# Attention scores computed transposed with the query maxima as an extra row, and convolution taps summed by GpSimd in the projections

## The chip, the cores and the metric

The kernel runs on one core of a Trainium2 chip. The core has five engines with queues of their own: TensorE (PE, matrix products, whose weight loads are PEld), VectorE (DVE), ScalarE (ACT), GpSimd (POOL) and SyncE (SP, which here only issues DMAs). They meet only through semaphores. The metric is the device time of one execution in microseconds. Measured before: a median of 2285.3 us over 3 runs (2282.73 to 2285.51).

## The reference

A two-layer encoder over 1024 tokens of width 1024, in float32. Each layer mixes tokens by latent attention of 8 heads beside a convolution over 31 positions on 512 channels, and then runs a gated feed-forward part with a convolution over 3 positions. Cut to what matters here:

```python
for l in range(DEPTH):
    h = _rmsnorm(x, g_mix[l])
    p = h @ w_in[l]
    q = (_rmsnorm(p[..., :o1], g_q[l]) @ w_uq[l]).reshape(b, s, MLA_HEADS, 64 + 32)
    kv = (_rmsnorm(p[..., o1:o2], g_kv[l]) @ w_ukv[l]).reshape(b, s, MLA_HEADS, 64 + 64)
    # q_rope, k_rope: the last 32 of q and p[..., o2:o3], rotated
    sc = einsum("bqhd,bkhd->bhqk", q_nope, k_nope) + einsum("bqhr,bkr->bhqk", q_rope, k_rope)
    y_attn = einsum("bhqk,bkhd->bqhd", softmax(sc * scale, axis=-1), v)
    a, gt = jnp.split(p[..., o3:], 2, axis=-1)
    u = _dwconv(a * sigmoid(gt), w_dw_conv[l], b_dw_conv[l])      # 31 taps
    u = silu(_layernorm(u, g_conv_ln[l], b_conv_ln[l]))
    x = x + concatenate([y_attn, u], axis=-1) @ w_o[l]
    z = _dwconv(_rmsnorm(x, g_ffn[l]) @ w_up[l], w_dw_ffn[l], b_dw_ffn[l])   # 3 taps
    zg, zv = jnp.split(z, 2, axis=-1)
    x = x + (silu(zg) * zv) @ w_down[l]
return _rmsnorm(x, g_final)
```

## The kernel before

Everything is kept transposed: channels on the 128 partitions, 1024 tokens along the free dimension. Each float32 operand of a product is split into an upper part, rounded to the PE's float32r format, and the remainder, and a product is three matmuls: upper by upper, upper by lower and lower by upper. The split is made by a cast on ACT and a subtraction on DVE. The order of PE, DVE, ACT and POOL is written out by hand; DMAs are issued from SP's queue (`move`) or from POOL's.

**Projections** (`project`, lines 516 to 819). The loop at line 801 walks through sections: gates and values of the convolution (four channel groups of 128), the latent parts, shared key, keys, rotated and plain queries. Each section's result stands in one of three two-bank PSUM tiles until DVE and ACT have taken it out. A planner keeps two clocks, PE's and DVE's: `work` (529) lets DVE do what a section needs as it falls due and fills the rest with taps of the 31-position convolution (`conv_step`, 1692: one multiply-add over 1024 tokens, 112 in all, NEAR_TAPS of 30 for each group). The other taps of a group are in `away`. Some go to `tap_far` (1697) in the longer sections: ACT multiplies, and a DMA from POOL's queue adds the product to the group's sum. Weights come in by DMAs on POOL's queue too: `cast` (161) loads the upper part, `complete` (177) has ACT negate it and adds the source by a second DMA (L174, L179). At the end queries and keys, upper and lower, go to DRAM, by head.

**Attention** (`attention`, 1469 to 1683). `load_head` brings back the four tiles of a head, queries and keys with 96 rows each. The main loop (1644) makes 64 steps, eight query tiles of eight heads. A step `n` issues: `scores` (1492) with queries as weights, six matmuls into a tile of 128 queries by 1024 keys, and DVE's maximum over the row; `expo` (1505), ACT's exponential with that maximum as bias and the row sum as a by-product; `turn` (1514), eight PE transposes a step of 128 by 128, since the product with the values needs keys on the partitions, with ACT's cast and DVE's subtraction of each half out of PSUM; and `values` (1537), four matmuls a step. `sums` (1567) turns a head's row sums, takes reciprocals and spreads them over 64 partitions by two DMAs through DRAM; POOL multiplies and splits the heads' results. `rows` (1476) makes the values' tiles at the start. The taps still in `away`, 49 a layer, are done during the steps by `tap_late` (1703): POOL or ACT multiplies, and POOL or a DMA adds. `early` and `finish` start the output product (`wo_steps`, 876) in the last steps.

PSUM has eight banks. In attention two two-bank tiles hold scores and four single banks the transposes, values and small things. SBUF tiles come from tagged pools: 31 of "b", 8 of "m" (heads' queries and keys), 3 of "wr" (exponentials), 8 of "ws".

**Feed-forward** (`feed`, 843) follows, and hands the next layer's first sections over.

## Time and profile before

| | |
|---|---|
| median of 3 runs | 2285.3 us |
| profiled execution, span from first to last instruction | 2282.9 us (the page gives no other time for it) |
| layer 0: projections, stretch 40 to 199 us | 159 us |
| layer 0: rows and attention, 199 to 424 us | 225 us |
| layer 1: rows and attention, 1326 to 1554 us | 228 us |
| granted TensorE clock | 0.999 |
| matmuls of scores, values, transposes (both layers) | 768, 512, 1024 |

The page gives busy time by engine, a strip of 40 slices, DMA queues, the chain that ended last, and the costliest groups of instructions. Matmuls overlap, so that the mean of one (389 ns) is longer than the distance from one to the next; the pitch is read from starts. In a tile's or line's rows the three figures are the shortest, median and longest duration in ns. In a timeline, two instructions merged into a row ("x2") have one duration for both. Idle time of an engine counts only where others wait for it.

### The profile page before, as it was taken

Reading aid. Unit: us, or ns where it says so; the run is one execution under the profiler, and the core shown is the slowest. Engines: PE = TensorE matmul, PEld = TensorE weight load, DVE = VectorE, ACT = ScalarE, POOL = GpSimd, SP = SyncE. Lnnn points to the kernel's source line nnn. Section 1 sums busy time; section 2 is a strip of 40 time slices with the busy share of each in tenths; the row PEclk is TensorE's granted clock in tenths of the full one; section 3 lists DMA queues with packets and bytes.
Section 4 is the critical chain, followed back from the end, with each engine's and each line's share of the span. In section 5 each row is a group of like instructions: output and inputs, shape, how many; then the busy total and the mean of one; then the engine's idle time right before and its main releaser. Section 6 shows DMA issues by size and latency. Waiting matters only on the chain.

```text
span 2282.9 us, 30530 instructions
## 1 busy us (share of the span) xinstructions
PE 2269.7 (99%) x10684; PEld 1887.8 (83%) x10684; DVE 1730.2 (76%) x2329; ACT 1286.7 (56%) x2043; POOL 781.8 (34%) x810
## 2 busy tenths in 40 slices
PE   9999999999999999999999999999999999999998
PEld 7888888888888888888888888888888888888887
DVE  6989888768877776776559788886697777768665
ACT  5445877646655555544533468774475555555444
POOL 1222787522333333001412237873323333320032
PEclk9999999999999999999999999999999999999999
DMA  6889998946899998935968999967659999989356
GB/s 185 165 175 271 194 200 166 235 138 145 211 277 296 275 296 208 334 106 143 209 136 166 218 255 197 184 149 207 175 129 228 271 302 279 294 210 315 102 124 167
DMA packets 198569, 475.73 MB, mean 208 GB/s; under 512 B 27296, under 2 KB 34576, under 8 KB 198416
## 3 DMA queue, kind: packets, MB, share of 16 engines
q0 software_dynamic: 103136, 222.46, 48.5%
...
## 4 chain that ended last, share of the span: by engine, by line
PE 92%; DVE 3%; DMA 1%; POOL 1%; ACT 1%; issue 1%; SPq 0%; DVEq 0%; ACTq 0%; POOLq 0%
PE p L1063 36%; PE pd L1251 18%; PE s L1500 7%; PE po L874 7%; PE o L1552 4%; PE t L1529 4%; PE pa L215 2%; PE pg L215 2%; PE pg L513 2%; DVE conv L1694 2%; PE pq L215 1%; PE pn L215 1%; PE pv L1481 1%; PE pkv L215 1%; PE pa L513 1%
## 5 line engine op out<-in xcount | busy, mean ns | idle before, releaser
L1063 PE MATMUL p<-b,w 128*128 128x512 f32 x3552 | 806.3, 389 | 0.1
L1063 PEld LDWEIGHTS p<-b,w 128*128 128x128 f32 x3552 | 666.4, 188 | 139.3 <-DVE w L1441 0.5
L1251 PE MATMUL pd<-ab,wd 128*128 128x512 f32 (+1 forms) x1920 | 422.3, 381 | 0.0
L1251 PEld LDWEIGHTS pd<-ab,wd 128*128 128x128 f32 x1920 | 350.7, 188 | 69.5 <-DVE ab L1441 0.4
L1500 PE MATMUL s<-k,q 96*128 96x512 f32 x768 | 208.0, 406 | 0.0
L179 POOL DMA_DIRECT2D w<-wu x96 | 84.7, 883 | 360.0 <-ACT w L178 319.1
L1532 DVE TENSOR_TENSOR pt<-t,pt 128x512 fp32r<-128x512 f32 x256 | 164.8, 685 | 53.6 <-ACT pt L1531 51.7
L1711 POOL TENSOR_TENSOR late<-gate,par 128x1018 f32<-128x1018 f32 (+12 forms) x79 | 171.7, 2174 | 18.7 <-issue 9.7
L1531 ACT CAST pt<-t 128x512 fp32r<-128x512 f32 x256 | 137.6, 589 | 65.2 <-PE t L1529 63.6
L1453 DVE SCALAR_TENSOR_TENSOR o<-zg,par,o 128x1023 f32<-128x1023 f32 x88 | 112.7, 1283 | 75.6 <-ACT o L1447 74.3
L179 POOL DMA_DIRECT2D w<-in_w_up x116 | 100.5, 866 | 199.4 <-ACT w L178 175.4
L1502 DVE TENSOR_REDUCE mx<-s 128x1 f32<-128x1024 f32 x128 | 155.8, 1217 | 0.0
L1500 PEld LDWEIGHTS s<-k,q 96*128 96x128 f32 x768 | 135.1, 189 | 22.9 <-ACT p L1510 0.2
L1510 ACT ACTIVATE p<-s,mx 128x1024 f32<-128x1024 f32 x128 | 144.8, 1131 | 1.9 <-DVE mx L1502 1.9
L1694 DVE SCALAR_TENSOR_TENSOR conv<-gate,par,conv 128x1009 f32<-128x1009 f32 (+7 forms) x112 | 142.3, 1274 | 3.6 <-ACT conv L575 1.0
L1552 PE MATMUL o<-pt,v 128*128 128x512 f32 x512 | 140.3, 397 | 0.0
L837 POOL DMA_DIRECT2D wd<-in_w_down x44 | 32.6, 744 | 307.9 <-PE pd L1251 306.9
L1439 ACT CAST ab<-ac 128x512 fp32r<-128x512 f32 x130 | 80.1, 617 | 98.3 <-DVE ac L1186 95.6
L178 ACT ACTIVATE w<-w 128x512 fp32r<-128x512 f32 x212 | 133.6, 630 | 3.0
L1529 PEld LDWEIGHTS t<-ident,p 128*128 128x128 f32 x1024 | 119.6, 140 | 18.5 <-ACT p L1510 1.2
L1529 PE MATMUL t<-ident,p 128*128 128x128 f32 x1024 | 133.3, 273 | 0.7 <-ACT p L1510 0.7
L1012 DVE TENSOR_TENSOR zg<-p,zg 128x512 f32<-128x512 f32 x88 | 60.5, 690 | 96.5 <-PE p L1063 89.6
...
## 6 DMA issues: line engine op xcount, KB each, us to landing
w<-in_w_up POOLq DMA_DIRECT2D x232, 256.0 KB, 7.2
...
w<-wu POOLq DMA_DIRECT2D x96, 256.0 KB, 5.9
...
wd<-in_w_down POOLq DMA_DIRECT2D x88, 256.0 KB, 5.3
...
ac<-act SPq DMA_DIRECT2D x72, 256.0 KB, 6.1
```

What stands on the lines that cost most here:

```text
L179: self.nc.gpsimd.dma_start(out=lo, in_=src, accum_op=ALU.add)
L215: nc.tensor.matmul(ps[:, HALVES[c]], w, x[:, HALVES[c]], start=(k == 0 and s == 0), stop=(k == n - 1 and s == 2))
L874: self.nc.tensor.matmul(ps, p[:, sl], q[:, cs], start=(k == 0 and t == 0), stop=(k == 3 and t == 2))
L1063: nc.tensor.matmul(ps, w[p][:, k * 128:(k + 1) * 128], b[:, q], start=(i in (1, 5, 2) and k == 0 and t == 0), stop=(k == 3 and t == 2), sk ...
L1251: nc.tensor.matmul(ps[t, m][:, cs], w[i, j][p][:, m * 128:(m + 1) * 128], b[:, q, cs], start=(i in (1, 5, 2) and j == 0 and s == 0), stop= ...
L1500: nc.tensor.matmul(ps[:, cs], q[i][0:96, qs], k[j][0:96, cs], start=(s == 0), stop=(s == 2))
L1502: nc.vector.tensor_reduce(out=mx, in_=ps, op=ALU.max, axis=AX.X, negate=True)
L1529: nc.tensor.transpose(tp[:, i, qi * 128:(qi + 1) * 128], st["p"][2 * qp + qi][:, kt * 128:(kt + 1) * 128], self.ident)
L1532: nc.vector.tensor_tensor(out=lo, in0=tp, in1=hi.bitcast(F32), op=ALU.subtract)
L1552: nc.tensor.matmul(po, v[2 * c + i][:, h // 2, e, :], pt[s][:, i, :], start=(c == 0 and i == 0 and s == 0), stop=(c == 3 and i == 1 and s ...
L1694: self.nc.vector.scalar_tensor_tensor(out=y[:, lo:hi], in0=u[:, lo + s:hi + s], scalar=self.tap(l, j, t), in1=y[:, lo:hi], op0=ALU.mult, o ...
L1711: self.nc.gpsimd.tensor_tensor(out=p[:, lo:hi], in0=u[:, lo + s:hi + s], in1=self.tap(l, j, t).broadcast_to([128, hi - lo]), op=ALU.mult)
```

## The change

In attention the score product is transposed: keys are the weights and queries move, so that a tile of 128 keys by 1024 queries comes out, with keys on the partitions as the value product needs them. PE's transposes go. The maximum of each query is found ahead of time from the upper parts alone (`peak`): two matmuls for every eighth query of a head, and DVE's maximum. A head's eight maxima go to DRAM and come back as row 96 of the query tile, beside a row of ones in the key tile, so that the last of the three score products subtracts them (97 rows). The exponential then needs no bias. It lies in SBUF, where ACT casts it (`cast`), DVE subtracts (`rest`: both operands in SBUF) and POOL adds the eight tiles of a head (`add`). `sums` turns these into row sums by eight matmuls with a column of ones. `peak` runs 12 steps ahead of the values, and 12 maxima come before the first scores, between the `rows`. Upper and lower tiles of a head are loaded apart. Head 1 gets its upper tiles directly, like head 0.

In the projections POOL takes taps from the end of `away` (`pool_tap`), up to ten for each group as the planner's clock allows, 3.4 us each: a product by a new one-operand form (`pool_product`) and an addition to the group's side sum, which one DMA adds to the group's sum in the end. What is left is done late, in turn by POOL and ACT, and in both cases added by a DMA. Four blocks of the output product instead of two begin in the last steps. The core of the diff (in `peak` to `sums`, in `spread` and `divide` and in the loop the removed lines are left out; they stand above):

```diff
-LATE_KINDS = (("pool", "both", "act", "pool", "act"), ("pool", "both", "pool", "pool", "pool"))
-LATE_COST = {"act": 1.1, "pool": 3.5, "both": 4.8}
+LATE_KINDS = ("pool", "act", "pool", "act")
+LATE_FROM = 0
+POOL_TAP = 3.4
+POOL_TAPS = (10, 10, 10, 10)
...
-DIRECT = 1
+DIRECT = 2
...
-        krd = [self.dp.tile([ROPE, T], F32R, name=f"krd{l}{i}") for i in range(2)]
+        krd = [self.dp.tile([ROPE + 1 - i, T], F32R, name=f"krd{l}{i}") for i in range(2)]
...
-            self.move(krd[0], krh[0:32, :])
+            self.move(krd[0][0:ROPE], krh[0:32, :])
+            self.move(krd[0][ROPE:ROPE + 1].rearrange("o (a b) -> (o a) b", a=8), self.ones_r[0:8, :])
...
+        pool_at, side = 0.0, {"j": 0, "n": 0}
+
+        def pool_tap():
+            j, y = side["j"], side.get("y")
+            t = away[j].pop()
+            lo, hi, s = self.span(t)
+            p = self.blk(f"side{l}_{j}_{t}")
+            if y is None:
+                side["y"] = p
+                if hi - lo < T:
+                    edge = p[:, hi:T] if hi < T else p[:, 0:lo]
+                    nc.gpsimd.memset(edge, 0.0)
+            self.pool_product(p[:, lo:hi], u[j][:, lo + s:hi + s], self.tap(l, j, t))
+            if y is not None:
+                nc.gpsimd.tensor_tensor(out=y[:, lo:hi], in0=y[:, lo:hi], in1=p[:, lo:hi], op=ALU.add)
+            side["n"] += 1
+            if side["n"] == POOL_TAPS[j] or not away[j]:
+                pool_merge()
+
+        def pool_merge():
+            j, y = side["j"], side.pop("y")
+            nc.gpsimd.dma_start(out=conv[j], in_=y, accum_op=ALU.add)
+            side.update(j=j + 1, n=0)
...
-            for j in sorted(far, key=far_at.get)[:FAR_TOGETHER if times[name] > 5.0 else 0]:
+            chosen = sorted(far, key=far_at.get)[:FAR_TOGETHER if times[name] > 5.0 else 0]
+            while pool_at + POOL_TAP <= clock["pe"] and away.get(side["j"]):
+                pool_at = max(pool_at, clock["pe"] - times[name]) + POOL_TAP
+                pool_tap()
+            for j in chosen:
                 self.tap_far(l, j, away[j].pop(0), u[j], conv[j])
...
+        if "y" in side:
+            pool_merge()
...
-        with self.psum(f"attn{l}", 2, 4):
+        with self.psum(f"attn{l}", 0, 2):
...
-            ms = (2 * i, 2 * i + 1) if n else ()
+            ms = (2 * i, 2 * i + 1) if n > 1 else ()
...
+    def upper_tiles(self, l, h):
+        return [self.tmp("m", f"{n}{l}_{h}0", F32R) for n in "qk"]
+
+    def lower_tiles(self, l, h):
+        return [self.tmp("m", f"q{l}_{h}1", F32R), self.tmp("ws" if h else "b", f"k{l}_{h}1", F32R)]
+
+    def load_part(self, l, h, p, qd, qrd, kd, krd):
+        q, k = tiles = self.lower_tiles(l, h) if p else self.upper_tiles(l, h)
+        self.move(q[0:NOPE, :], qd[p][h])
+        for i in range(2):
+            self.move(q[NOPE + i * HALF:NOPE + (i + 1) * HALF, :], qrd[p][i, h])
+        self.move(k[0:NOPE, :], kd[p][h])
+        rows = ROPE if p else ROPE + 1
+        self.move(k[NOPE:NOPE + rows, :], krd[p][0:rows])
         return tiles
...
+        def wide(name, tag):
+            return self.pp.tile([128, T], F32, name=name, tag=tag, bufs=2 if tag == "st" else 1)
...
+        def peak(h, i, tag="sm"):
+            st = state[h]
+            if i == 0:
+                st["mx"] = self.cp.tile([128, 8], F32R, name=f"mx{l}_{h}", tag="mx", bufs=2)
+            q, k = upper[h]
+            ps = wide(f"m{l}_{h}_{i}", tag)
+            for cs in HALVES:
+                nc.tensor.matmul(ps[:, cs], q[0:96, i::8], k[0:96, cs], start=True, stop=True)
+            nc.vector.tensor_reduce(out=st["mx"][:, i:i + 1], in_=ps, op=ALU.max, axis=AX.X, negate=True)
+            if i == 7:
+                self.move(md[h].rearrange("(p i) -> p i", i=8), st.pop("mx"))
+                self.move(q[96:97, :], md[h:h + 1])
+
         def scores(n):
+            h, kt = divmod(n, 8)
+            (qh, kh), (ql, kl) = upper[h], lower[h]
+            ks = slice(kt * 128, kt * 128 + 128)
+            ps = state[h]["s", kt] = wide(f"s{l}_{h}_{kt}", "st")
+            for s, (k, q, rows) in enumerate(((kh, ql, 96), (kl, qh, 96), (kh, qh, 97))):
+                for cs in HALVES:
+                    nc.tensor.matmul(ps[:, cs], k[0:rows, ks], q[0:rows, cs], start=s == 0, stop=s == 2)
+            if kt == 7:
+                upper.pop(h), lower.pop(h)
+
+        def expo(n):
+            h, kt = divmod(n, 8)
             st = state[h]
+            p = st["p", kt] = self.tmp("b" if kt % 4 == 3 else "wr", f"p{l}_{h}_{kt}")
+            nc.scalar.activation(out=p, in_=st.pop(("s", kt)), func=AF.Exp)
+
+        def cast(n):
+            h, kt = divmod(n, 8)
             st = state[h]
+            st["pt", kt] = [self.tmp("ws", f"pt{l}_{h}_{kt}{i}", F32R) for i in range(2)]
+            nc.scalar.copy(out=st["pt", kt][0], in_=st["p", kt])
+
+        def rest(n):
+            h, kt = divmod(n, 8)
             st = state[h]
+            hi, lo = st["pt", kt]
+            nc.vector.tensor_tensor(out=lo, in0=st["p", kt], in1=hi.bitcast(F32), op=ALU.subtract)
+
+        def add(n):
+            h, kt = divmod(n, 8)
             st = state[h]
+            if kt == 0:
+                return
+            if kt == 1:
+                st["acc"] = self.blk(f"acc{l}_{h}")
+            a = st.pop(("p", 0)) if kt == 1 else st["acc"]
+            nc.gpsimd.tensor_tensor(out=st["acc"], in0=a, in1=st.pop(("p", kt)), op=ALU.add)
+
+        def values(n):
+            h, kt = divmod(n, 8)
+            st, e = state[h], h % 2
+            if kt == 0:
+                st["po"] = [self.bank(f"o{l}_{h}_{c}") for c in range(2)]
+                if e == 0:
+                    st["y"], st["rb"] = self.blk(f"yt{l}_{h}"), self.blk(f"rb{l}_{h}")
+                else:
+                    st["y"], st["rb"] = state[h - 1]["y"], state[h - 1]["rb"]
+            pt = st.pop(("pt", kt))
+            for c, cs in enumerate(HALVES):
+                for s in range(2):
+                    nc.tensor.matmul(st["po"][c], v[kt][:, h // 2, e, :], pt[s][:, cs],
+                                     start=kt == 0 and s == 0, stop=kt == 7 and s == 1)
+
+        def sides(h):
             e = h % 2
+            return slice(e * 64, e * 64 + 64), slice(64 - e * 64, 128 - e * 64)
+
+        def gather(h, c):
+            main, aux = sides(h)
+            y, ps = state[h]["y"][main, HALVES[c]], state[h]["po"][c]
+            nc.scalar.copy(out=y, in_=ps[aux, :])
+            nc.vector.tensor_tensor(out=y, in0=ps[main, :], in1=y, op=ALU.add)
+
+        def sums(h):
+            st = state[h]
+            (main, _), acc = sides(h), st.pop("acc")
+            ps = wide(f"sr{l}_{h}", "st" if h == last else "sm")[:, 0:8]
+            for i in range(8):
+                cols = slice(i * 128, i * 128 + 128) if h == last else slice(i, T, 8)
+                nc.tensor.matmul(ps[:, i:i + 1], acc[:, cols], self.ones[:, 0:1], start=True, stop=True)
+            rs = self.cp.tile([128, 8], F32, name=f"rs{l}_{h}", tag="rs", bufs=2)
+            nc.vector.reciprocal(out=rs, in_=ps)
+            if h == last:
+                return rs
+            y, rb = st["y"], st["rb"]
+            nc.sync.dma_start(out=sd[h].rearrange("(p i) -> p i", i=8), in_=rs)
             nc.sync.dma_start(out=rb[main, :], in_=sd[h:h + 1].partition_broadcast(64))
...
+        def spread(r):
+            ps = wide(f"rc{l}", "st")
+            for i in range(8):
+                nc.tensor.transpose(ps[:, i * 128:i * 128 + 128], r[:, i:i + 1].broadcast_to([128, 128]), self.ident)
+            return ps
+
+        def divide(ps, c):
+            main, _ = sides(last)
+            y = state[last]["y"][main, HALVES[c]]
+            nc.vector.tensor_tensor(out=y, in0=ps[main, HALVES[c]], in1=y, op=ALU.mult)
 
...
+            kind = LATE_KINDS[i % len(LATE_KINDS)]
+            n, steps = LATE_FROM + (SIDE_TIME - LATE_FROM) * i // len(late), self.tap_late(l, j, t, u[j], conv[j], kind)
+            for e in range(2 if kind == "act" else 1):
+                agenda[n + e].append(lambda steps=steps: next(steps, None))
...
+        load = lambda h, p: self.load_part(l, h, p, *spill)
+
+        def begin(n):
+            scores(n)
+            expo(n)
+
+        tags = ("st", "st", "sm")
+        for i in range(8):
+            peak(0, i, tags[i % 3])
+            if i % 2:
+                rows(i // 2)
+        for i in range(4):
+            peak(1, i)
+            rows(4 + i)
+        for n in (0, 1):
+            begin(n)
+            cast(n)
+            rest(n)
+            add(n)
+        for n in range(total):
+            h, kt = divmod(n, 8)
+            if kt == 0 and h:
+                sums(h - 1)
+            if n + 2 < total:
+                begin(n + 2)
+            g, i = divmod(n + 12, 8)
+            if g < HEADS:
+                peak(g, i)
             if n == total - 2:
+                early(0, range(3))
             if n == total - 1:
+                early(1, range(3))
+                r = sums(last)
+            values(n)
+            if kt == 7:
+                if n == total - 1:
+                    r = spread(r)
+                    early(2, range(3))
+                for c in range(2):
+                    gather(h, c)
+                    if n == total - 1:
+                        divide(r, c)
+                        if c == 0:
+                            finish(state[last]["y"], 0)
             if n + 2 < total:
+                cast(n + 2)
+                rest(n + 2)
+                add(n + 2)
+            g, i = divmod(n + 15, 8)
+            if i == 0 and g < HEADS:
+                upper[g] = load(g, 0)
+            g, i = divmod(n + 5, 8)
+            if i == 0 and g < HEADS:
+                lower[g] = load(g, 1)
             for f in agenda.pop(n, ()):
                 f()
+        early(3, range(3))
...
+            self.nc.scalar.activation(out=p[:, lo:hi], in_=u[:, lo + s:hi + s], func=AF.Copy, scale=self.tap(l, j, t))
+            yield
...
+            self.pool_product(p[:, lo:hi], u[:, lo + s:hi + s], self.tap(l, j, t))
...
+    def pool_product(self, out, src, tap):
+        self.nc.gpsimd.tensor_scalar(out=out, in0=src, scalar1=tap, scalar2=1.0, op0=ALU.mult, op1=ALU.mult)
```

201 lines of the change are left out of this document (31 added, 170 removed).

## Prediction

> **What bounds the kernel now.** I read the page first: the busy line, then the chain that ended last.
>
> ```profile
> span 2282.9 us, 30530 instructions
> PE 2269.7 (99%) x10684; PEld 1887.8 (83%) x10684; DVE 1730.2 (76%) x2329; ACT 1286.7 (56%) x2043; POOL 781.8 (34%) x810
> ...
> PE 92%; DVE 3%; DMA 1%; POOL 1%; ACT 1%; issue 1%; SPq 0%; DVEq 0%; ACTq 0%; POOLq 0%
> ```
>
> PE holds 99% of the span: whatever shortens PE's list shortens the kernel, as long as no other engine becomes the limit. So I cut the span into stages (columns: stretch, length, then busy time and count of PE, PEld, DVE, ACT, POOL).
>
> ```profile
> core 0: us, PE busy (x) PEld busy (x) DVE busy (x) ACT busy (x) POOL busy (x), PEclk, DMA share, GB/s
> 40.00:199.00 159.00, 158.11 (x713) 130.54 (x712) 141.93 (x158) 69.47 (x71) 35.14 (x42) 1.00 0.82 175
> 230.00:390.00 160.00, 160.00 (x907) 135.31 (x906) 134.72 (x169) 128.15 (x231) 130.91 (x85) 1.00 0.89 188
> ```
>
> The first stretch is layer 0's projections: DVE is busy 141.9 of 159 us, so it has some 17 us to give, and POOL only issues DMAs. The second is the attention loop. Its 907 matmuls at 18 a step make 50.4 steps, 3.175 us each, 203 us for 64. One step in PE's timeline:
>
> ```profile
> 271.62 1.63 PE L1500 MATMUL s<-k,q 96*128 96x512 f32 x6
> 273.08 1.10 PE L1552 MATMUL o<-pt,v 128*128 128x512 f32 x4
> 274.02 1.04 PE L1529 MATMUL t<-ident,p 128*128 128x128 f32 x8
> 274.81 1.41 PE L1500 MATMUL s<-k,q 96*128 96x512 f32 x5
> ```
>
> From start to start: 1.46 us for six score matmuls, 0.94 for four value matmuls, 0.79 for eight transposes. The chain over the projections gives the plain pitch:
>
> ```profile
> 42.98 10.88 PE pa L215 x48
> ```
>
> 10.88/48 = 0.227 us for a 512-column matmul.
>
> **PE's part of the change.** A step loses the transposes (0.79) and gains two maximum matmuls. Twelve matmuls at 0.227 are 2.72; the breaks between groups now cost about 0.10 and 0.03 (1.46 and 0.94 less 6 and 4 pitches), so I take 0.15 for three groups: 2.87. The row sums are eight one-column matmuls a head; this row prices them at 1.9/16 = 0.12:
>
> ```profile
> L236 PE MATMUL rf_1p<-ones,fss 128*128 128x1 f32 x16 | 1.9, 239 | 0.0
> ```
>
> That is 0.96 a head, 0.12 a step: 2.99 against 3.175. If PE stays the bound, attention gains 64 x 0.18 = 11 us a layer, 23 in all.
>
> **Who else must keep up.** ACT trades accumulate reads and two half casts for one whole cast, about as much as before, and stays under. DVE trades two 0.68 us subtractions from PSUM for one whole one, but its operands change: p and its upper part both lie in SBUF, where before one lay in PSUM. At the same time POOL adds the exponentials of seven of eight steps, and in the projections multiplies and adds taps while DVE runs its own. So I looked for places where POOL's arithmetic met such a DVE instruction (columns: start, duration).
>
> ```profile
> 202.78 2.04 POOL L1711 TENSOR_TENSOR late<-gate,par 128x1020 f32<-128x1020 f32 x1 [9.02 <-DMA qrd<-qr]
> 202.99 2.91 DVE L710 SCALAR_TENSOR_TENSOR qn<-qn,qns 128x1024 fp32r<-128x1024 f32 x1
> L710 DVE SCALAR_TENSOR_TENSOR qn<-qn,qns x8: 1215/1218/2912, 193.9 to 1331.6; 128x1024 fp32r<-128x1024 f32 x8
> 415.29 2.39 POOL L1722 TENSOR_TENSOR lns<-lns,conv 128x1024 f32<-128x1024 f32 x1
> 417.00 1.23 DVE L1608 SCALAR_TENSOR_TENSOR ys_7l<-yt,ys_7h 128x512 fp32r<-128x512 f32 x1 [0.69 <-ACT ys_7h L1607]
> 505.54 1.22 DVE L922 TENSOR_TENSOR fss<-fss,fss 128x1024 f32<-128x1024 f32 x1
> 505.71 3.46 POOL L1441 TENSOR_TENSOR b<-y,b 128x512 fp32r<-128x512 f32 x2 [1.06 <-ACT b L1439]
> L1441 POOL TENSOR_TENSOR b<-y,b x16: 1289/1608/2206, 491.9 to 1637.6; 128x512 fp32r<-128x512 f32 x16
> L1532 DVE TENSOR_TENSOR pt<-t,pt x256: 671/682/693, 214.8 to 1548.5; 128x512 fp32r<-128x512 f32 x128
> ```
>
> L710 usually takes 1.22 us. Here POOL had started 0.21 earlier and ended at 204.82; L710 ended at 205.90, 1.08 after it. L1608 ends 0.55 after POOL's end at 417.68. The other way round, POOL's 1.29 us operation took 2.21 when DVE's two-SBUF addition had 1.05 left. So they do not share: the later one waits for the whole of the first, then needs its free time less 0.14. L1532, with one operand in PSUM, never varies (671 to 693), though POOL worked beside it all along. The Trainium skill, SBUF — State Buffer, section Who interferes with whom, calls this an exclusive lock on a read port that the two engines share; by it nothing here changes in the sum, but a reduction from PSUM stays free of it.
>
> That speaks against the change: I count the time for which the port is held, which cannot overlap.
>
> **Projections.** DVE's instructions with two SBUF operands, by line in the stretch 40 to 203:
>
> ```profile
> L1694 DVE SCALAR_TENSOR_TENSOR conv<-gate,par,conv 128x1009 f32<-128x1009 f32 (+14 forms) x56 | 71.1, 1273 | 1.3 <-ACT conv L575 0.2
> ...
> L568 DVE TENSOR_TENSOR gate<-gate,rx 128x1024 f32<-128x1024 f32 x4 | 4.9, 1224 | 4.3 <-ACT gate L566 4.3
> ...
> L640 DVE TENSOR_TENSOR krt<-krt,krt 32x1024 f32<-32x1024 f32 x1 | 1.2, 1206 | 0.0
> ```
>
> 56 taps and 29 others (lines 568 to 710 but for those that read PSUM): 85, at 1.08 held = 92 us. Following the planner's clock, POOL gets 37 taps a layer (ten for each of three channel groups, seven for the last), far taps stay at 15 and about 12 of 49 remain late. POOL's prices:
>
> ```profile
> L1711 POOL TENSOR_TENSOR late<-gate,par x79: 1861/2182/2581, 202.8 to 1519.8; 128x1013 f32<-128x1013 f32 x8, 128x1012 f32<-128x1012 f32 x8, 128x1011 f32<-128x1011 f32 x8, 128x1010 f32<-128x1010 f32 x8
> L1714 POOL TENSOR_TENSOR conv<-conv,late x20: 2358/2382/2410, 208.0 to 1517.5; 128x1016 f32<-128x1016 f32 x3, 128x1010 f32<-128x1010 f32 x3, 128x1018 f32<-128x1018 f32 x2, 128x1021 f32<-128x1021 f32 x2
> L1700 ACT ACTIVATE far<-gate,par x30: 1129/1136/1155, 87.1 to 1285.7; 128x1023 f32<-128x1023 f32 x10, 128x1021 f32<-128x1021 f32 x8, 128x1022 f32<-128x1022 f32 x8, 128x1020 f32<-128x1020 f32 x4
> ```
>
> An addition holds 2.38 - 0.13 = 2.25. The new one-operand product is in no row: at most the old product's 2.18 (L1711), at least about ACT's 1.13. The planner's 3.4 a tap, less 2.38, leaves 1.0; half the two-operand addition is 1.2, and I take 1.2, held 1.07. The Trainium skill, GPSIMD Engine Reference, section Engine selection, has one-input operations roughly at line rate; an estimate from it would be the same, and no run here shows it. Held by POOL: 33 additions (the first tap of a group has none) x 2.25 + 37 x 1.07 = 114 us. With DVE's 92: 206 us. The port can serve from DVE's first tap to the first row matmul:
>
> ```profile
> L1694 DVE SCALAR_TENSOR_TENSOR conv<-gate,par,conv x112: 1253/1274/1285, 48.5 to 1275.2; 128x1009 f32<-128x1009 f32 x8, 128x1010 f32<-128x1010 f32 x8, 128x1011 f32<-128x1011 f32 x8, 128x1012 f32<-128x1012 f32 x8
> L1481 PEld LDWEIGHTS pv<-wv0h,kvs_0h x8: 188/188/188, 199.2 to 215.2; 128*128 128x128 f32 x8
> ```
>
> 151 us: **55 too few**. It does not matter who loses: behind a waiting DVE stand the evictions that free PE's three wide PSUM tiles; behind a waiting POOL stand the weights' DMAs (L174, L179), in one queue with the taps. PE waits for both. +55 a layer, +110.
>
> **Attention.** A head holds the port for 7 additions x 2.25 + 8 subtractions x 1.08 = 24.4 us; eight heads 195, six multiplications and splits of y at about 2.4 on POOL 14, six late products 6: 215, or 3.37 a step. This exceeds PE's 2.99 and the old 3.175: +13 a layer, +26. DVE's maxima run while POOL adds. Buffers are behind it: exp needs a tile that POOL's addition frees, and PE needs exp to free the score tile.
>
> **Prologue and tail.** Twelve maxima come ahead of the first scores: 12 x 1.22 on DVE, and rows 16 x 0.41, 21 us against PE's 72 x 0.227 = 16; then the maxima go through DRAM in two DMAs, where the like pair for the sums takes 4.7 us for its second half:
>
> ```profile
> rb<-sd SPq DMA_DIRECT2D x14, 256.0 KB, 4.7
> L1502 DVE TENSOR_REDUCE mx<-s x128: 1204/1215/1225, 207.8 to 1537.9; 128x1 f32<-128x1024 f32 x128
> L1489 DVE TENSOR_TENSOR v<-pv,v x32: 406/414/426, 205.8 to 1347.7; 128x256 fp32r<-128x256 f32 x32
> ```
>
> The rows and maxima of head 1 cover most of it; I take +5 a layer (0 to 10), +10. The upper tiles of head 1 are filled by further moves on SP's queue, inside that. The tail reorders the same matmuls: 0, bounds -3 to +3 a layer.
>
> Sum: 110 + 26 + 10 = 146. The profiled span lies 2.4 us under the median of the runs, 0.1%; on 2285.3 that gives **2431 us**, say 2430. With additions held for 2.0 and products for 0.9 the projections give +39 and attention -2 a layer: 2370. With the product at 2.18, 43 products x 0.98 add 84: 2515.
>
> **Rivals.**
> - *Projections bind, attention does not* (adds slip into gaps at other moments): 2285 + 110 - 23 = 2372. For it: POOL's DMA issues leave room.
> - *PE stays the bound*, the faster side: DVE and POOL overlap after all. Then -23 and a covered prologue: 2263. It decides where a tap on POOL holds the port less than (151 - 92)/37 = 1.6 us, half of my 3.1. Against it stand the waits above, in both layers.
> - *Strided weights*: the maximum matmuls load every eighth column, which no row shows; contiguous loads take 0.188 (L1481). Up to 0.41 each PE's spare 0.37 a step hides it; at four times, 0.75, a step grows by 0.67, +43 a layer: 2516. The Trainium skill, SBUF — State Buffer, section Door 1: The DMA port swizzle, says that accesses crossing a 16-byte line each time are penalised; it gives no price, and no run here shows it.
> - *Dear product*, 2.18: 2515.
>
> **Chances.** Both stages bound by the port 0.50 (2390 to 2490), projections alone 0.16, dear product 0.10, strided weights 0.07, PE the bound 0.13, all cancelling 0.04. Slower by over 0.2% (4.6 us, about what a measurement can tell) 0.83, within 0.04, faster 0.13. The range 2300 to 2520 leaves out the last two cases and 0.03 above.
>
> **What would show it.** Right: L1694's mean well over 1.27 and spread, POOL's additions over 2.4, PE idle in the projections behind DVE and POOL, the projections near 210 us, steps near 3.4. Wrong: L1694 still at 1253 to 1285 while POOL multiplies, PE at 99%, steps at 3.0. If maximum matmuls lie further apart than 0.23 with nobody to wait for, it is the strided loads; if PE waits only at each layer's first scores, it is the maxima's way through DRAM.

## Result and the profile after

The changed kernel takes 2616.7 us (median of 4 runs, 2616.1 to 2618.8) against 2284.6: ratio 1.1457, 95% interval 1.1441 to 1.1473. That is 332 us more; 146 were forecast and the range ended at 2520. First the page: span, busy line, the chain that ended last by engine and by line.

```profile
span 2614.9 us, 29263 instructions
...
PE 2399.0 (92%) x10158; PEld 1957.0 (75%) x10158; DVE 2019.7 (77%) x2199; ACT 1256.6 (48%) x1760; POOL 1197.9 (46%) x938
...
PE 63%; DVE 20%; issue 7%; POOL 4%; ACT 3%; DMA 3%; SPq 1%; DVEq 0%; POOLq 0%; ACTq 0%
PE p L1097 29%; PE pd L1285 16%; DVE conv L1752 8%; PE po L908 6%; DVE pt L1575 3%; DVE mx L1543 3%; PE s L1555 3%; PE sr L1618 2%; POOL acc L1585 2%; PE pg L515 1%; PE o L1599 1%; PE m L1542 1%; ACT p L1563 1%; PE pa L217 1%; PE pa L515 1%
```

PE was busy 99% of the span and is now at 92%; DVE carries 20% of the chain (3% before), with the convolution's taps (L1752), the subtraction (L1575) and the maxima (L1543) in it. Next the stages of layer 0: projections, what comes ahead of attention, attention; then the old attention (columns as before: stretch, length, busy time and count of PE, PEld, DVE, ACT, POOL, granted clock, DMA share, GB/s).

```profile
40.00:281.00 241.00, 173.71 (x712) 139.67 (x711) 228.59 (x160) 68.67 (x71) 188.33 (x118) 0.86 0.60 126
281.00:308.00 27.00, 22.80 (x73) 17.51 (x73) 24.94 (x29) 6.49 (x16) 6.11 (x3) 0.77 0.86 298
308.00:593.00 285.00, 253.21 (x929) 200.87 (x927) 225.98 (x152) 156.65 (x166) 219.41 (x106) 0.88 0.40 97
```

```profile
204.00:422.00 218.00, 217.64 (x1219) 183.62 (x1218) 182.96 (x239) 172.11 (x315) 163.41 (x111) 1.00 0.90 206
```

The 712 matmuls of the projections (713 in the stretch 40 to 199 before) now end at 281. DVE is busy 228.6 of 241 us, PE idles 67, and the granted clock is 0.86. Attention has 929 matmuls instead of 1219 and yet takes 285 us instead of 218: PE idles 32, and 253 us busy over 929 matmuls are 0.27 us each. The old loop had 0.18, with the short transposes in it; its 512-column matmuls went at 0.23 to 0.24. The bounds of each stage, read from single instructions (minimum/median/maximum ns, first and last start):

```profile
L1542 PEld LDWEIGHTS m<-k,q x256: 312/328/347, 280.7 to 1823.4; 96*128 96x128 f32 x128
```

```profile
L1555 PEld LDWEIGHTS s<-q,k x768: 186/188/337, 307.6 to 1857.7; 96*128 96x128 f32 x128, 97*128 97x128 f32 x64
```

```profile
L1797 PEld LDWEIGHTS lnp<-lns0h,ones_r x2: 186/262/338, 593.1 to 594.4; 128*128 128x128 f32 x2
```

```profile
L1500 PE MATMUL s<-k,q x768: 387/393/479, 203.5 to 1537.2; 96*128 96x512 f32 x192
```

```profile
L1738 PE MATMUL lnp<-lns0h,ones_r x2: 392/396/400, 422.3 to 422.8; 128*128 128x512 f32 x2
```

Layer 0 begins its first row or maximum at 280.7 instead of 199.2 (+82), goes from there to its first scores in 26.9 us instead of 4.3 (+23), and from these to the end of attention in 285.5 instead of 218.8 (+67). The page's groups show the prediction's first sign:

```profile
L1585 POOL TENSOR_TENSOR acc<-acc,p 128x1024 f32<-128x1024 f32 x96 | 273.1, 2845 | 102.7 <-ACT p L1563 99.4
L1575 DVE TENSOR_TENSOR pt<-p,pt 128x1024 fp32r<-128x1024 f32 x128 | 292.5, 2289 | 30.7 <-ACT pt L1569 29.1
...
L1752 DVE SCALAR_TENSOR_TENSOR conv<-gate,par,conv 128x1009 f32<-128x1009 f32 (+7 forms) x112 | 247.0, 2209 | 3.6 <-ACT conv L577 1.0
...
L798 POOL TENSOR_TENSOR side<-side,side 128x1010 f32<-128x1010 f32 (+8 forms) x66 | 192.1, 2911 | 5.5
```

L1752 has a mean of 2.21 us (1.27 before), the subtraction 2.29 (one-operand ones took 0.68 a half), POOL's additions 2.85 and 2.91 (2.38 before). What PE waited for in the projections (columns: us in total, times, longest):

```profile
PE rkv0s L286 <- DVE rkv0y L271: 18.1, 1, 18.1
```

The longest wait is for the keys' root, nine DVE instructions on 128x8 values. DVE's timeline there (start, duration):

```profile
199.67 2.17 DVE L265 TENSOR_TENSOR rkv0t<-rkv0y 128x8 f32<-128x8 f32 x1
201.88 1.04 DVE L266 TENSOR_TENSOR rkv0t<-rkv0t,rkv0v 128x8 f32<-128x8 f32 x1
202.96 0.17 DVE L267 SCALAR_TENSOR_TENSOR rkv0t<-rkv0t 128x8 f32<-128x8 f32 x1
...
206.45 0.17 DVE L270 SCALAR_TENSOR_TENSOR rkv0t<-rkv0t,rkv0v 128x8 f32<-128x8 f32 x1
206.65 2.18 DVE L271 SCALAR_TENSOR_TENSOR rkv0y<-rkv0t,rkv0y 128x8 f32<-128x8 f32 x1
```

Each of these took 0.17 us before. All seven from L265 to L271 have two operands in SBUF (L265, L267 and L269 the same tile twice), so the operands do not explain why two of those shown still take 0.17. What differs is what POOL does at that moment:

```profile
201.80 1.11 POOL L1775 TENSOR_SCALAR side<-gate,par 128x1013 f32<-128x1013 f32 x1
202.99 2.32 POOL L798 TENSOR_TENSOR side<-side,side 128x1013 f32<-128x1013 f32 x1
```

L266 ends with POOL's product (201.80 + 1.11 = 202.91). L267 starts at 202.96, before the addition at 202.99, and takes 0.17; L270 falls into the next such gap. The others wait for a product or an addition to end, 1.04 to 2.18 us. An exclusion that lasts a whole instruction charges a tiny one the full length of the other.

### The profile page after: what moved, and what is told of

Read it like the earlier page. It is cut to its first block, busy times and chain, and to the rows that moved or that the text cites. A ratio compares the mean times of both kernels' runs of the same rounds, so it can differ in the third digit from the quotient of the medians.

```text
span 2614.9 us, 29263 instructions
## 1 busy us (share of the span) xinstructions
PE 2399.0 (92%) x10158; PEld 1957.0 (75%) x10158; DVE 2019.7 (77%) x2199; ACT 1256.6 (48%) x1760; POOL 1197.9 (46%) x938
## 4 chain that ended last, share of the span: by engine, by line
PE 63%; DVE 20%; issue 7%; POOL 4%; ACT 3%; DMA 3%; SPq 1%; DVEq 0%; POOLq 0%; ACTq 0%
PE p L1097 29%; PE pd L1285 16%; DVE conv L1752 8%; PE po L908 6%; DVE pt L1575 3%; DVE mx L1543 3%; PE s L1555 3%; PE sr L1618 2%; POOL acc L1585 2%; PE pg L515 1%; PE o L1599 1%; PE m L1542 1%; ACT p L1563 1%; PE pa L217 1%; PE pa L515 1%
## 5 line engine op out<-in xcount | busy, mean ns | idle before, releaser
L1585 POOL TENSOR_TENSOR acc<-acc,p 128x1024 f32<-128x1024 f32 x96 | 273.1, 2845 | 102.7 <-ACT p L1563 99.4
L1575 DVE TENSOR_TENSOR pt<-p,pt 128x1024 fp32r<-128x1024 f32 x128 | 292.5, 2289 | 30.7 <-ACT pt L1569 29.1
L1752 DVE SCALAR_TENSOR_TENSOR conv<-gate,par,conv 128x1009 f32<-128x1009 f32 (+7 forms) x112 | 247.0, 2209 | 3.6 <-ACT conv L577 1.0
L1555 PE MATMUL s<-q,k 96*128 96x512 f32 (+1 forms) x768 | 226.1, 434 | 7.3 <-DMA k<-krd 5.5
L1563 ACT ACTIVATE p<-s 128x1024 f32<-128x1024 f32 x128 | 130.9, 1023 | 208.1 <-PE s L1555 96.4
L1555 PEld LDWEIGHTS s<-q,k 96*128 96x128 f32 (+1 forms) x768 | 160.7, 212 | 47.2 <-issue 5.2
L798 POOL TENSOR_TENSOR side<-side,side 128x1010 f32<-128x1010 f32 (+8 forms) x66 | 192.1, 2911 | 5.5
L1543 DVE TENSOR_REDUCE mx<-m 128x1 fp32r<-128x1024 f32 x128 | 154.7, 1214 | 45.9 <-PE m L1542 45.9
L1775 POOL TENSOR_SCALAR side<-gate,par 128x1009 f32<-128x1009 f32 (+9 forms) x74 | 132.3, 1796 | 10.1 <-DMA kd<-kh 9.0
L1569 ACT CAST pt<-p 128x1024 fp32r<-128x1024 f32 x128 | 134.5, 1051 | 3.8
```

Source lines behind the costliest of these rows:

```text
L798: nc.gpsimd.tensor_tensor(out=y[:, lo:hi], in0=y[:, lo:hi], in1=p[:, lo:hi], op=ALU.add)
L1543: nc.vector.tensor_reduce(out=st["mx"][:, i:i + 1], in_=ps, op=ALU.max, axis=AX.X, negate=True)
L1555: nc.tensor.matmul(ps[:, cs], k[0:rows, ks], q[0:rows, cs], start=s == 0, stop=s == 2)
L1563: nc.scalar.activation(out=p, in_=st.pop(("s", kt)), func=AF.Exp)
L1575: nc.vector.tensor_tensor(out=lo, in0=st["p", kt], in1=hi.bitcast(F32), op=ALU.subtract)
L1585: nc.gpsimd.tensor_tensor(out=st["acc"], in0=a, in1=st.pop(("p", kt)), op=ALU.add)
```

## Experiments

Runs on the same chip were compared with the kernel before in each group (2283.5 to 2284.3 us). In every diff, lines of the changed kernel are the minus side unless it says otherwise.

**The two halves alone.** `taps_only` is the kernel before with the projections' part put in (`pool_tap`, `pool_merge`, the product and their calls, as in the change's diff):

```diff
+POOL_TAP = 3.4
+POOL_TAPS = (10, 10, 10, 10)
...
+            while pool_at + POOL_TAP <= clock["pe"] and away.get(side["j"]):
+                pool_at = max(pool_at, clock["pe"] - times[name]) + POOL_TAP
+                pool_tap()
```

`attn_only` is the changed kernel with

```diff
-POOL_TAP = 3.4
+POOL_TAP = 1e9
```

> The kernel before with only the projections' part of the change (products and additions of 37 taps of a layer on POOL; attention as before, with fewer late taps). Theory A, the two parts add up: the changed kernel's layer 0 reaches its values' rows 82 us later than before, so 2 x 82 = 164 us, less up to 20 for the late taps that attention no longer carries: 2430 to 2450 us. Theory B, the two parts amplify each other through the clock (0.943 granted against 0.999): clearly under half of the 332 us, 2395 us or less, which is also what the prediction's 110 us for this part would give.

> The changed kernel without POOL's taps in the projections: those 37 taps of a layer become late taps beside the transposed attention. Theory A: 2284.6 + 2 x (66 in attention + 13 ahead of it) = 2443 us, and up to 30 more for the added late taps, so 2440 to 2475. Theory B: below 2400. If the projections' loss came from something other than POOL's work there, the first row matmul of layer 0 would stay near 280 us; with theory A it is back near 199.

Measured: 2446.2 us, ratio 1.0706 (1.0690 to 1.0722), and 2484.9 us, 1.0876 (1.0860 to 1.0892). So the projections' part costs 162 us, and the rest of the change 2616.7 - 2446.2 = 170. `attn_only` lies 10 above its range. If the two parts add up, its 37 more late taps a layer cost 2484.9 + 162 - 2616.7 = 30, the top of what was allowed for them; no run shows that price alone. Theory B, amplification through the clock, falls: each part alone costs more than it allowed.

**What in the projections.** Four kernels on the base of `taps_only` (the minus side). `write_only`, with POOL as busy but reading nothing:

```diff
-            self.pool_product(p[:, lo:hi], u[j][:, lo + s:hi + s], self.tap(l, j, t))
-            if y is not None:
-                nc.gpsimd.tensor_tensor(out=y[:, lo:hi], in0=y[:, lo:hi], in1=p[:, lo:hi], op=ALU.add)
+            nc.gpsimd.memset(p[:, lo:hi], 0.0)
+            for _ in range(2 if y is not None else 0):
+                nc.gpsimd.memset(y[:, lo:hi], 0.0)
```

> The kernel before with the projections' part alone, but POOL's products and additions replaced by writes of zeros into the same tiles (one for a product, two for an addition), so that POOL is busy and its queue is full but it reads nothing; those taps are left out of the result. Theory A, DVE's two-SBUF instructions exclude POOL's reads: the taps of L1726 fall from 2.24 to about 1.3 us, the small root instructions to 0.2, and the time to 2285 to 2310. Rival, POOL's full queue delays the weights that it issues: 2400 or more.

Measured: 2332.0 us, 1.0204 (1.0188 to 1.0220), above theory A's 2285 to 2310 and far below the rival's 2400. Layer 0's writes on POOL, then the taps on DVE, then ACT's wait for the tile of a far tap (both layers), and one of the first two instructions of the keys' root in layer 1:

```profile
L797 POOL MEMSET side<- 128x1010 f32 (+8 forms) x66 | 70.8, 1072 | 1.9
L795 POOL MEMSET side<- 128x1009 f32 (+9 forms) x37 | 43.7, 1211 | 1.1 <-DMA k<-kl 1.1
```

```profile
L1726 DVE SCALAR_TENSOR_TENSOR conv<-gate,par,conv x112: 1253/1275/1289, 48.2 to 1316.7; 128x1009 f32<-128x1009 f32 x8, 128x1010 f32<-128x1010 f32 x8, 128x1011 f32<-128x1011 f32 x8, 128x1012 f32<-128x1012 f32 x8
```

```profile
ACT far L1732 <- DMA conv<-far: 37.4, 9, 8.5
```

```profile
1309.93 2.99 DVE L264 TENSOR_SCALAR rkv1y<-rkv1v 128x8 int32<-128x8 int32 x1
```

POOL is as busy as the sum had it (114.5 us, against 37 products and 33 additions forecast at 114), and the taps are back at 1253 to 1289 ns. 114 of the 162 us go with the reads. That a write does not count is also what the Trainium skill says (SBUF — State Buffer, section Who interferes with whom: a DVE instruction with two SBUF inputs contends with a GpSimd instruction that reads SBUF, not with one that only writes it); this run agrees for the taps and for the roots' two-operand instructions, which all take 0.17 us again. It is not so for the roots' first two, L263 and L264, with one operand: beside POOL's writes and DMA issues the keys' pair took 0.88 and 0.96 us in layer 0, and L264 2.99 in layer 1, against 0.17 to 0.26 before. 48 us stay, and here the trace points to POOL's queue: ACT waits 37.4 us for the tiles of far taps, against 4.8 in the kernel before, and DVE once waits 8.0 us for a far transfer, for which it has no such wait before. So the rival seems to hold in part; no run changes the queue alone.

`products_only` drops the addition, `half_taps` halves the pace, `held` keeps POOL out of the stretch in which DVE had no gap:

```diff
-                nc.gpsimd.tensor_tensor(out=y[:, lo:hi], in0=y[:, lo:hi], in1=p[:, lo:hi], op=ALU.add)
...
-POOL_TAP = 3.4
+POOL_TAP = 6.8
...
+            if name in ("kv0", "kv1", "kr", "q0", "q1", "q2"):
+                pool_at = clock["pe"]
             while pool_at + POOL_TAP <= clock["pe"] and away.get(side["j"]):
```

> The kernel before with the projections' part alone, POOL's products kept (37 a layer) and its additions left out (only one product of a row is added to the convolution). POOL then reads 37 x 1.10 = 41 us a layer instead of 41 + 33 x 2.25 = 115. If the loss goes with the time that POOL reads, past what DVE has free: 162 us x 41 / 115 = 58, 2330 to 2345. If every POOL instruction costs DVE one wait whatever its length, half of it stays: 2365 or more.

> The kernel before with the projections' part alone and half as many POOL taps (one for each 6.8 us of TensorE's work instead of 3.4; the others go to attention as late taps). POOL reads about 57 us a layer. If the loss goes with that time: 162 x 57 / 115 = 80, 2355 to 2375. If DVE has slack for the first half, 2320 or less; if any POOL work across the small root instructions costs the whole stall there, 2400 or more.

> The kernel before with the projections' part alone, POOL taps at the changed kernel's pace but none while the sections kv0 to q2 run (the stretch from 97 us to the root of the keys, in which DVE has no idle time before): 20 taps a layer, 12 ahead of the stretch and 8 behind it, POOL reads 20 x 1.1 + 18 x 2.25 = 62 us. If loss goes with the time that POOL reads wherever it falls (81 us a layer for 115, 29 for 40 with 13 taps), it is 44 a layer: 2370. If only reads in the full stretch count, DVE's idle time outside (15 us ahead of it) takes some: 2320 or less. Above 2350 the place does not matter.

Measured: 2331.0 us, 1.0209 (1.0194 to 1.0224); 2341.7 us, 1.0254 (1.0239 to 1.0270); 2363.5 us, 1.0347 (1.0330 to 1.0364). `half_taps` missed its range: its trace has 13 products and 11 additions a layer, not the 18 taps reckoned with, so POOL reads 39 us there, not 57. `held` lies close to the 2370 of its first branch and above the 2350 from which the place does not matter: keeping POOL out of the full stretch saves little. The price of a product, from the changed kernel's shortest:

```profile
L1775 POOL TENSOR_SCALAR side<-gate,par x74: 1104/2052/3146, 55.0 to 1576.8; 128x1009 f32<-128x1009 f32 x8, 128x1010 f32<-128x1010 f32 x8, 128x1011 f32<-128x1011 f32 x8, 128x1012 f32<-128x1012 f32 x8
```

With 1.10 a product and 2.25 an addition, and the loss a layer as half the difference of the times:

| run | POOL reads, us a layer | loss measured | port: 92 + reads - 151 | DVE's list: 142 + reads - 159 | DVE busy, layer 0 | projections longer, layer 0 |
|---|---|---|---|---|---|---|
| products_only | 41 | 24 | 0 | 24 | 164.5 | 17 |
| half_taps | 39 | 29 | 0 | 22 | 169.5 | 27 |
| held | 63 | 40 | 4 | 46 | 182.7 | 42 |
| taps_only | 115 | 81 | 56 | 98 | 224.7 | 80 |
| write_only | 0 | 24 | 0 | 0 | 146.4 | 20 |

The port column is the prediction's rule; the next takes all of DVE's 141.9 busy us of the stretch 40 to 199. The last two columns are read from the traces, from 40 us to the first row matmul's weight load (199.2 before); a busy DVE includes its waits for the port. The line for `taps_only`:

```profile
40.00:278.70 238.70, 176.22 (x713) 141.91 (x712) 224.69 (x158) 68.86 (x70) 185.61 (x117) 0.85 0.60 126
```

The prediction's rule does not follow the measurements. DVE's own time does: where POOL reads, DVE's busy time grows by 23, 28, 41 and 83 us, the projections by 17, 27, 42 and 80, and DVE idles 12 to 19 us of the stretch, as before (17). DVE works its list in order: while an instruction waits for POOL, the evictions and reductions behind it, which do not need the port, wait too. The list with its waits sets the length of the stage. Not every microsecond that POOL reads becomes such a wait, only 55 to 72%, and the idle 17 us are not used up; in the fifth column these two errors cancel for the small reads, and for 115 us they leave 17 too much. `write_only` is of another kind: DVE is busy 146.4 of 179 us there, and the stage is as late for other reasons. The queue is not excluded in the other rows either, but it is smaller: in `products_only` ACT waits 9.3 us for far tiles in the two layers, 4.5 more than before the change.

In `half_taps` PE waits 10.1 us for the keys' root although eight of its nine instructions take 0.17 to 0.20 us there; they only start late:

```profile
PE rkv0s L286 <- DVE rkv0y L271: 10.1, 1, 10.1
```

So the slow root instructions are a small part; the lateness is gathered by the whole list. In `taps_only` some of the 81 us may be the queue (ACT waits 30.4 us there); this was not separated.

**What in attention.** From here the base is the changed kernel. `no_adds` keeps the first of POOL's seven additions, `few_sums` one of eight sums, `lean` both (where additions are missing, an addition of 1 stands in place of the sums' reciprocal):

```diff
-            a = st.pop(("p", 0)) if kt == 1 else st["acc"]
-            nc.gpsimd.tensor_tensor(out=st["acc"], in0=a, in1=st.pop(("p", kt)), op=ALU.add)
+            b = st.pop(("p", kt))
+            if kt == 1:
+                nc.gpsimd.tensor_tensor(out=st["acc"], in0=st.pop(("p", 0)), in1=b, op=ALU.add)
...
-            for i in range(8):
+            for i in range(8 if h == last else 1):
```

> The changed kernel with POOL's additions of the exponentials left out from the third tile on (row sums of two tiles only, one added before the reciprocal). Theory P, the port and POOL's lag set attention: the subtraction falls from 2.29 to 1.21 us, steps fall from 4.2 us to about 3.6 (twelve matmuls 2.72, strided loads 0.2, sums 0.5), 0.6 x 128 steps = 75 us gained: about 2540. Theory Q, TensorE's own additions (strided loads, sums of 3.94 us a head, half clock behind them) set it: 0 to 25 us gained, 2590 to 2617.

> The changed kernel with one of the eight sums of a head instead of eight (its column used for all eight; the last head keeps its own). Theory Q, TensorE's added work sets attention: 14 heads x 3.4 us = 48 us and up to 20 for the half clock behind them: 2550 to 2570. Theory P, the exclusion of DVE's subtraction and POOL's addition sets it and TensorE waits for the last addition here anyway: under 20 us gained, 2597 to 2617. (The run with two wide matmuls took 42 us more than the changed kernel, with 14 reciprocals of 6.55 us = 92 us new on DVE: 50 us would be gained beside them by Q, if DVE's 92 us count in full.)

> The changed kernel without POOL's additions from the third tile on and with one of the eight sums of a head (the last head keeps its eight; one is added in place of the reciprocal). Alone the first gave 78 us and the second 48. If the two are separate costs, 2617 - 126 = 2491; if both only take away the same waits of TensorE, 2535 or so. What then is left above the run with the projections' part alone (2446) is the price of the order ahead of attention (2 x 13 = 26) and of strided loads and other waits (some 20).

Measured: 2538.4 us, 1.1108 (1.1089 to 1.1126); 2568.5 us, 1.1246 (1.1229 to 1.1262); 2485.4 us, 1.0886 (1.0868 to 1.0904). The additions are worth 78 us, the sums 48, together 131: nearly separate costs. Without additions the subtraction is back:

```profile
L1575 DVE TENSOR_TENSOR pt<-p,pt 128x1024 fp32r<-128x1024 f32 x128 | 167.0, 1304 | 71.2 <-ACT pt L1569 70.0
```

Where the time goes is seen in the steps. DVE's timeline of the changed kernel in a step inside a head, then PE's around the sums at a head's end:

```profile
366.56 2.28 DVE L1575 TENSOR_TENSOR pt<-p,pt 128x1024 fp32r<-128x1024 f32 x1
368.77 1.21 DVE L1543 TENSOR_REDUCE mx<-m 128x1 fp32r<-128x1024 f32 x1
369.90 2.28 DVE L1575 TENSOR_TENSOR pt<-p,pt 128x1024 fp32r<-128x1024 f32 x1
```

```profile
371.67 1.56 PE L1555 MATMUL s<-q,k 96*128 96x512 f32 x6
373.37 0.87 PE L1542 MATMUL m<-k,q 96*128 96x512 f32 x2
374.07 1.09 PE L1599 MATMUL o<-pt,v 128*128 128x512 f32 x4
375.73 3.93 PE L1618 MATMUL sr<-ones,acc 128*128 128x1 f32 x16 [0.56 <-DVE mx L1543]
379.52 2.90 PE L1555 MATMUL s<-q,k 96*128 96x512 f32 x6
...
383.08 1.91 PE L1599 MATMUL o<-pt,v 128*128 128x512 f32 x4
```

Inside a head, while POOL adds without a break, its addition (2.25 held) and DVE's subtraction (1.08 held) take turns, and DVE's maximum runs under the addition: 369.90 - 366.56 = 3.34 us from one subtraction to the next, as 2.25 + 1.08 has it, and PE's step goes with them. From the starts of the value matmuls in layer 0, 20 of the 56 steps inside heads take 3.30 to 3.45 us and 14, where POOL is not adding, 2.79 to 2.92; the mean is 3.55. The seven steps across a head's end, where the sums stand, take 8.9 to 11.2 us (here 383.08 - 374.07 = 9.01), 68 together; ahead of the sums PE waits 6.0 us a layer for maxima and 5.1 for POOL's last additions. Against 3.175 a step that is 21 us more inside the heads and 46 at their ends, the 67 that attention has become longer. Without additions (`no_adds`) most steps inside are 2.80 and six of the seven ends still 8.8 to 8.9; with one sum (`few_sums`) the seven ends take 44.

The sums cost what they last: sixteen passes (two for each matmul) take 3.8 us, and 14/16 of that in 14 heads is 46. Behind them six score matmuls take 2.90 instead of 1.56 and four value matmuls 1.91 instead of 1.09: for some 5 us PE goes at half pace. The granted clock is 1.00 from 375.7 to 377.5 and 0.50 from 379.5 to 385.0; its mean over the stage is 0.88. The Trainium skill (TensorE: Matmul & The Clock Gate, section HAM oscillation — how this bites in real kernels) describes a clock that falls to half when a wait between short bursts of matmuls outlasts some 3.4 us. The trace does not show that case here: PE waited only 0.56 us ahead of the sums. That matmuls of one column count as little work is a guess, which no run tests alone; `few_sums` gained 48 us in all, hardly more than the passes' 46.

In `lean` the loop takes 528.6 - 305.2 = 223 us of layer 0, near the old 219:

```profile
L1555 PEld LDWEIGHTS s<-q,k x768: 186/188/331, 305.2 to 1729.3; 96*128 96x128 f32 x128, 97*128 97x128 f32 x64
```

```profile
L1798 PEld LDWEIGHTS lnp<-lns0h,ones_r x2: 186/188/189, 528.6 to 529.8; 128*128 128x128 f32 x2
```

Above `taps_only` 39 us are left. In the 26.9 us that the changed kernel has ahead of the first scores, where before 4.3 stood (19 matmuls at 0.227, three rows), there are also the other five rows, which ran inside the loop before (30 x 0.227 = 6.8). The other 16 a layer are 5.4 for the first maxima's 24 matmuls, 4.2 in which PE idles, and some 6.5 from PE's clock of 0.77 (22.8 us busy for 72 matmuls, 16.3 at 0.227). `lean` has the same 16. The last 7 us were not split.

**Two repairs that were none.** `wide_sums` makes the row sums with ones as weights, and `block_peaks` takes maxima over neighbouring queries:

```diff
-                nc.tensor.matmul(ps[:, i:i + 1], acc[:, cols], self.ones[:, 0:1], start=True, stop=True)
+                    nc.tensor.matmul(ps[:, cs], self.ones_r, acc[:, cs], start=True, stop=True)
+                nc.vector.reciprocal(out=rb[main, :], in_=ps[main, :])
...
-                nc.tensor.matmul(ps[:, cs], q[0:96, i::8], k[0:96, cs], start=True, stop=True)
+                nc.tensor.matmul(ps[:, cs], q[0:96, i * 128:i * 128 + 128], k[0:96, cs], start=True, stop=True)
...
+                    nc.tensor.transpose(tp, st.pop("mx").bitcast(F32), self.ident)
```

> The changed kernel with the eight sums of a head (sixteen passes with strided weights, 3.94 us) made by two F32R matmuls with ones as weights and the added exponentials moving, 0.45 us, a reciprocal of 64x1024 on DVE, and no transfer for the spread, in all heads but the last. Theory Q: 14 heads x 3.5 us = 49 us, and up to 14 x 2 for the half clock behind them: 2540 to 2570. Theory P: TensorE waits at this place for POOL's last addition anyway, so under 20 us gained, 2597 to 2617.

> The changed kernel with the maxima taken over blocks of 128 neighbouring queries (weights with neighbouring columns) and put in row order by one transposition of 128x8 a head. Theory Q: two weight loads a step at 0.188 instead of 0.33 us, up to 0.2 us x 112 steps = 22 us gained, less some 0.4 us x 14 for the transpositions: 2590 to 2605. Theory P: the loads lie beside waits, 2605 to 2625.

Measured: 2658.3 us, 1.1637 (1.1620 to 1.1654), and 2641.2 us, 1.1573 (1.1547 to 1.1599): both slower than the change and above every range set for them. A reciprocal of 64x1024 turned out to take 6.55 us:

```profile
L1624 DVE RECIPROCAL rb<-sr 64x1024 f32<-64x1024 f32 x14 | 91.7, 6549 | 0.2
```

92 us on DVE for 49 saved on PE is close to the 42 measured. `block_peaks` loads in 189 ns instead of 328, but its transposition waits for DVE's maximum:

```profile
PE mt L1547 <- DVE mx L1543: 12.4, 8, 3.2
...
PE m L1542 <- DVE mt L1549: 7.6, 4, 5.4
```

```profile
L1542 PEld LDWEIGHTS m<-k,q x256: 186/189/338, 281.1 to 1847.8; 96*128 96x128 f32 x128
```

12.4 + 7.6 us a layer of new waits behind DVE are 40 in all; 24.5 were lost, so by this sum the rest of the edit gained some 15. The maxima themselves wait in DVE's list behind subtractions that wait for POOL.

**Taking the second operand away.** `combo` has no POOL taps in the projections, block maxima, and sums as one row that ACT copies and transfers turn; above all it writes the exponential twice:

```diff
-            nc.scalar.activation(out=p, in_=st.pop(("s", kt)), func=AF.Exp)
-            nc.scalar.copy(out=st["pt", kt][0], in_=st["p", kt])
-            nc.vector.tensor_tensor(out=lo, in0=st["p", kt], in1=hi.bitcast(F32), op=ALU.subtract)
+            nc.scalar.activation(out=st["pt", kt][0], in_=st["s", kt], func=AF.Exp)
+            nc.scalar.activation(out=st["s", kt], in_=st["s", kt], func=AF.Exp)
+            nc.vector.tensor_tensor(out=lo, in0=st.pop(("s", kt)), in1=hi.bitcast(F32), op=ALU.subtract)
```

`combo2` goes back to every eighth query and has ACT multiply three of four late taps; `combo4` also loads the next head's lower tiles two steps earlier and moves three smaller things that are not printed here (the sums' transfers, the slots of the rounded exponentials, the output weights):

```diff
-            g, i = divmod(n + 5, 8)
+            g, i = divmod(n + 7, 8)
             if i == 0 and g < HEADS:
                 lower[g] = load(g, 1)
```

> No POOL taps in the projections; transposed attention in which the exponential is written both as the rounded tile and in place in PSUM, so that the subtraction has one SBUF operand; POOL adds the rounded tiles; maxima over blocks; sums as two wide F32R matmuls, one row copied by ACT and turned by transfers. Theory P: the subtraction is back at 1.21 us beside POOL's additions, TensorE sets the step at 2.95 to 3.1 us against 3.175 before, 64 steps gain 5 to 14 us a layer, and 13 a layer ahead of attention stay: 2270 to 2310. Rival, TensorE's own breaks and the clock hold the step near 3.6 us whatever the subtraction takes: 2340 or more.

> The run with the exponential in PSUM once more (2424), with the maxima over every eighth query as in the changed kernel (no transposition to wait for, 15 to 25 us) and three of four late taps multiplied by ACT instead of half of them (POOL was busy 18 to 19 of 20 us in attention there; 12 products a layer of 1.6 us each taken away, up to 38 us): 2365 to 2410. If POOL's queue is not the bound of that run, 2400 to 2415. Below 2284 it would beat both kernels; nothing here gives that much.

> The last run with the exponential in PSUM (2406; its steps are 2.81 us apart where nothing waits, against 3.175 before) with the breaks between heads taken away: lower tiles of the next head loaded two steps earlier and ahead of the sums' transfers, the rounded exponentials in other slots than the scores' tiles, the output weights cast two steps earlier. If transfers at the heads' ends are what is left (16.7 us a layer of waits for k and about as much in half-speed matmuls behind them): 2406 - 2 x 34 - 2 x 6 = 2326, range 2300 to 2350; 64 steps of 2.81 with the 24 us ahead of them would be 2290. If POOL's queue paces the steps, 2380 or more.

Measured: 2424.2 us, 1.0606 (1.0590 to 1.0622); 2406.0 us, 1.0537 (1.0521 to 1.0553); 2389.2 us, 1.0462 (1.0447 to 1.0478). `combo` lies far above the 2270 to 2310 of its theory P, but the first part of that theory held: the subtraction is at its free time with all seven additions beside it:

```profile
L1585 DVE TENSOR_TENSOR pt<-s,pt 128x1024 fp32r<-128x1024 f32 x128 | 156.5, 1223 | 71.9 <-ACT s L1579 61.1 <-POOL acc L1595 10.3
```

So it is the second SBUF operand, not POOL's presence. In `combo2`, PE's steps where nothing waits, and the loads of the maxima:

```profile
299.63 1.08 PE L1600 MATMUL o<-pt,v 128*128 128x512 f32 x4
300.55 1.56 PE L1556 MATMUL s<-q,k 96*128 96x512 f32 x6
301.95 0.64 PE L1543 MATMUL m<-k,q 96*128 96x512 f32 x2
302.43 1.08 PE L1600 MATMUL o<-pt,v 128*128 128x512 f32 x4
```

```profile
L1543 PEld LDWEIGHTS m<-k,q x256: 312/326/347, 200.9 to 1611.5; 96*128 96x128 f32 x128
```

302.43 - 299.63 = 2.80 us a step, below the prediction's 2.99, and the two maximum matmuls take 0.48 from start to next start although their strided loads take 326 ns: in a full stream these loads cost nothing. Behind a wait they do: the pair shown above for the changed kernel takes 374.07 - 373.37 = 0.70. Part of what held `combo2` up were transfers at each head's start:

```profile
PE s L1556 <- DMA k<-krd: 16.7, 7, 4.9
```

`combo4` took these waits away and gained 17 us, a fifth of the 80 expected. Its attention as one window, POOL's two largest groups in it, and what PE now waits for ahead of the sums:

```profile
240.00:440.00 200.00, 173.21 (x692) 138.72 (x692) 138.60 (x129) 165.78 (x180) 187.90 (x122) 0.95 0.92 188
```

```profile
L1586 POOL TENSOR_TENSOR acc<-acc,pt 128x1024 fp32r<-128x1024 f32 (+1 forms) x43 | 114.0, 2652 | 3.3 <-ACT pt L1564 2.5
L1788 POOL DMA_DIRECT2D conv<-late x49 | 51.4, 1081 | 8.8 <-DMA conv<-late 5.0 <-POOL late L1791 3.8
```

```profile
PE sr L1623 <- POOL acc L1586: 18.6, 6, 6.9
```

POOL is busy 188 of 200 us: additions 114 in this group, issues of late taps 51. With the port out of the way POOL's own list is the last to finish at the heads' ends, and 2389 is what was expected if it paces the steps (2380 or more); no run took work off it alone. No kernel run here reaches 2284 us; of those that leave nothing out `half_taps` comes nearest, 2.5% behind.

## Why the prediction was right in direction and wrong in size

- **Mechanism: right.** Two-operand DVE instructions and POOL's reads exclude each other. The reads removed (`write_only`, `no_adds`) or one operand moved to PSUM (`combo`), and the durations are back at 1.28, 1.30 and 1.22 us.
- **Projections, +110: measured 162.** The counts were right (37 products and 33 additions a layer) and so was the product's price (1.2 taken, 1.10 at its shortest). The step that failed is "The port can serve from DVE's first tap to the first row matmul" with its 151 us. It compared the time for which the port is held with the stage, as if DVE could do its other work while an instruction waits. In `taps_only` DVE's whole list with its waits takes 224.7 us, 83 more than before, and the stage is 80 longer, where 55 were forecast. Of the 162 us 114 go when POOL's reads go; for the other 48 the cause stays open, with POOL's queue as the likely one.
- **PE's step, 2.99 us: the sums were mis-sized.** "this row prices them at 1.9/16 = 0.12" was taken for a matmul, but the row L236 counts passes, two for each matmul in fp32: eight matmuls are sixteen rows, 1.9 us and not 0.96. And a pass took 0.24 us here, with strided weight loads of 335 ns in the median, where that row's are contiguous: 3.8 us a head. That is 48 us by `few_sums`, some 13 in the forecast. The rest of the step was even dear: 2.80 is seen.
- **Attention, +26 from the port: the step was right, the heads' ends were left out.** The turns of 2.25 and 1.08 us are seen inside the heads, where layer 0 loses 21 us against 13 forecast; the additions alone are worth 78 us. The capacity rule holds here because DVE's other work in a step, a maximum of 1.21 us, fits under one addition; in the projections DVE had no such room. At the heads' ends, for which the forecast had the sums' 0.96 us and no wait, the seven steps of layer 0 are 46 us longer than before; the sums, the half clock behind them and the waits for the last addition and the maxima meet there.
- **Prologue, +10: measured about 32** (16 a layer). It set DVE's maxima against PE's 16 us and put nothing for a clock of 0.77; 5 of the 16 a layer are the maxima's matmuls, which its steps already held.
- **Rivals.** Projections alone (2372) and PE as the bound (2263) fall: both parts cost. The dear product falls at 1.10. Strided weights were the right place for the sums; for the maxima a load of 0.33 us is hidden in a full stream, within the 0.41 allowed, and shows behind a wait.
